# Scores of two 64-dim heads on the two row halves of the matmul array, output products alternating between column halves

## The chip, the cores and the metric

The kernel runs on one core of one Trainium2 chip. The metric is the device time of one execution in microseconds (us). The engines are TensorE (PE: matmuls, with its weight loads listed as PEld), VectorE (DVE), ScalarE (ACT), GpSimd (POOL) and SyncE (SP, which issues most DMAs). TensorE multiplies with an array of 128 rows (the contraction) by 128 columns (the output partitions).

## What is computed

A transformer forward pass on 256 tokens of width 1024: a first block (mixing with attention and long convolutions, then a routed expert layer) and a second one (two layers with two feed-forward parts and one attention each). The change touches the three attentions. All have heads of 64 dimensions, and two heads lie together on 128 partitions. Cut to that:

```python
s = jnp.einsum('bqkgd,btkd->bkgqt', qblk, k) * scale      # mix: 8 query heads, 512 keys
p = softmax(s);  o = jnp.einsum('bkgqt,btkd->bqkgd', p, v)
...
logits = jnp.einsum('bqhmd,bkhmd->bhmqk', qb, k) * scale + bias   # diff: 8 heads, m = 2 maps of 64 dims
w = p[:, :, 0] - lam * p[:, :, 1];  o = jnp.einsum('bhqk,bkhe->bqhe', w, v)
...
logits = jnp.einsum('bqhd,bkhd->bhqk', qb, k) * scale + decay     # forget: 16 heads, causal
p = softmax(logits);  o = jnp.einsum('bhqk,bkhd->bqhd', p, v)
```

## The kernel before, in words

The program runs through nine phases (`PHASES`, line 47): mix, peer, f00, diff, f01, kv, f10, forget, f11. In each the big weights stream in from HBM, are split into a high and a low part (ACT writes `whi`, DVE writes `wlo`), and TensorE multiplies them with the activations, three fp32r products for one exact one (`mm_unit`, line 361). The attention work runs beside this as generators: `spawn` puts one on a list, and `tick`, called twice in each weight unit, takes every generator one step further, to its next `yield`. The framework's scheduler then sets the order of the instructions on each engine, by dependencies and priorities, so neighbours on TensorE need not be neighbours in the code. In the profile and in the orders below, `win`, `qkv`, `bq`, `pacc`, `kvu` and `gu` are such weight products in fp32r; the attention products are fp32. One fp32 product is two TensorE instructions in the trace and one row in the orders.

The attention parts that the change touches:

- `mix` (line 1232), `attn`: four pairs `t` of query heads, two query tiles `qt` of 128. Keys of both heads (256 tokens and 256 context tokens) lie in `kz`, which has one zero-padded copy for each head `m`: rows 0 to 63 hold the keys in copy 0, rows 64 to 127 in copy 1, the rest is zero (memset on POOL, line 1252; filled by `headnorm`, line 1088, in two pieces of 64 partitions). A score `sc` is one product over all 128 rows with 512 output columns. Softmax writes `E`, four transposes write `pt`, ACT copies it to `PT`. The output product `po` takes 64 columns of `V` as weights for each head, so head 0 fills output partitions 0 to 63 and head 1 fills 64 to 127: four products of 256 columns for head 0, then four for head 1.
- `diff` (line 724), `head`: eight heads with two maps `m`. Here the query side is padded: `qz` holds two copies with the other half zero (memsets at line 736, filled by two ACT instructions of 64 partitions for each head). The scores of both maps for one query tile go into one PSUM tile (`ps[:, m]`, from the pool `ps_x`, two buffers); one DVE instruction scales both and adds the bias. Products have 128 (`qt` 0) or 256 (`qt` 1) columns. Its `po` uses the whole array and is not changed.
- `forget` (line 1000), `pair`: eight pairs of heads, padded query copies as in `diff`, one DVE instruction for each head already. `po` has one product of 256 columns and one of 128 for each head, head 0 first.

The two copies with zeros are what lets one head's scores be computed on all 128 rows:

```python
ps = psx.tile([P, 2, nk], F32, tag="s", name="sc")
for m in range(2):
    nc.tensor.matmul(ps[:, m], qz[:, m, qt * P:(qt + 1) * P], k[:, :nk], start=True, stop=True)
```

Of the kernel before, what the change touches and what calls it, by code (L numbers as in the profile page):

```python
# [20 lines left out]
P = 128  # L21
T = 256
# [259 lines left out]
class Kern:  # L282
# [441 lines left out]
    def diff(self):  # L724
# [5 lines left out]
        with ExitStack() as es:  # L730
            pp = es.enter_context(self.tc.tile_pool(name="dfp", bufs=1))
            pw = es.enter_context(self.tc.tile_pool(name="dfw", bufs=2))
            psx = es.enter_context(self.tc.tile_pool(name="ps_x", bufs=2, space=PSUM))
            QZ = [pp.tile([P, 2, T], F32, name=f"qz{j}") for j in range(2)]
            for q in QZ:
                nc.vector.memset(q, 0.0)
            O = pp.tile([P, 2, NH, P], F32, name="O")
            SS = pp.tile([P, 2, NH], F32, name="SS")

            def head(h, qz, k, vf):  # L740
                pv = self.ps_bg.tile([P, 2, P], F32, tag="bg", name="vt")
                for t in range(2):
                    nc.tensor.transpose(pv[:, t], vf[:, t * P:(t + 1) * P], self.ident)
                V = pw.tile([P, 2, P], F32, tag="V", name="V")
                nc.scalar.activation(V, pv, AF.Copy)
                for qt in range(2):
                    nk = (qt + 1) * P
                    ps = psx.tile([P, 2, nk], F32, tag="s", name="sc")
                    for m in range(2):
                        nc.tensor.matmul(ps[:, m], qz[:, m, qt * P:(qt + 1) * P], k[:, :nk], start=True, stop=True)  # L750
                    L = pw.tile([P, 2, nk], F32, tag=f"L{qt}", name="L")
                    bias = self.dbias[:, h, T - nk:]
                    nc.vector.scalar_tensor_tensor(L, ps, 0.125, bias[:, None, :].to_broadcast([P, 2, nk]),
                                                   op0=ALU.mult, op1=ALU.add)
# [24 lines left out]
                    j = pw.tile([P, P], F32, tag="junk", name="junk")  # L779
                    nc.scalar.activation(j, O[:, qt, h], AF.Square, scale=2.0 ** -32, accum_out=SS[:, qt, h:h + 1])  # L780
# [3 lines left out]
            for h in range(NH):  # L784
                t3 = []
                qz = QZ[h % 2]
                for j in range(3):
# [8 lines left out]
                    if j == 0:  # L796
                        if h >= 2:
                            self.drain(*[g for g, n in last if n <= h - 2])
                        for m in range(2):
                            s = slice(m * 64, m * 64 + 64)  # L800
                            nc.scalar.activation(qz[s, m], ps[s], AF.Identity, bias=b[s] if early else 0.0)
                    else:
                        t = pw.tile([P, T], F32, tag=f"kv{j}", name="kvf")
                        if early:
# [195 lines left out]
    def forget(self):  # L1000
# [7 lines left out]
        with ExitStack() as es:  # L1008
            pp = es.enter_context(self.tc.tile_pool(name="fgp", bufs=1))
            pw = es.enter_context(self.tc.tile_pool(name="fgw", bufs=2))  # L1010
            psx = es.enter_context(self.tc.tile_pool(name="ps_x", bufs=2, space=PSUM))
            QZ = [pp.tile([P, 2, T], F32, name=f"qz{j}") for j in range(2)]
            for q in QZ:
                nc.vector.memset(q, 0.0)
            oh, ol = self.hh, self.hl

            def pair(t, qz):
                E2 = [pw.tile([P, 2, (qt + 1) * P], F32, tag=f"E{qt}", name="E") for qt in range(2)]
                for qt in range(2):
                    nk = (qt + 1) * P  # L1020
                    ps = psx.tile([P, 2, nk], F32, tag="s", name="sc")
                    for m in range(2):
                        h = 2 * t + m
                        nc.tensor.matmul(ps[:, m], qz[:, m, qt * P:(qt + 1) * P], self.K[:, t, :nk],
                                         start=True, stop=True)
                    L = pw.tile([P, 2, nk], F32, tag=f"L{qt}", name="L", bufs=1)
                    for m in range(2):
                        h = 2 * t + m
                        nc.vector.scalar_tensor_tensor(L[:, m], ps[:, m], self.F8[:, qt, h:h + 1],
                                                       (self.Fb if qt else self.Fa)[:, h],  # L1030
                                                       op0=ALU.add, op1=ALU.add)
                    sm = pw.tile([P, 8], F32, tag="sm", name="sm", bufs=4)
# [20 lines left out]
                        nc.vector.tensor_copy(WT[:, m], pt)  # L1053
                yield
                po = self.ps_bg.tile([P, T], F32, tag="bg", name="po")
                for m in range(2):
                    h = 2 * t + m
                    s = slice(h * 64, h * 64 + 64)
                    w = WT[:, m].rearrange("p a b -> p (a b)")
                    r = slice(m * 64, m * 64 + 64)  # L1060
                    nc.tensor.matmul(po[r], self.V[:, 0, s], w[:, :T], start=True, stop=False)
                    nc.tensor.matmul(po[r, P:], self.V[:, 1, s], w[:, T:], start=False, stop=True)
                self.split(po, oh[:, t], ol[:, t])
                yield

# [2 lines left out]
            for t in range(8):  # L1068
# [5 lines left out]
                qz = QZ[t % 2]  # L1074
                if t >= 2:
                    self.drain(gens[t - 2])
                for m in range(2):
                    s = slice(m * 64, m * 64 + 64)
                    nc.scalar.activation(qz[s, m], q[s], AF.Identity, bias=b[s])
# [152 lines left out]
    def mix(self):  # L1232
        nc, tc = self.nc, self.tc
        with ExitStack() as es:
# [11 lines left out]
            S = self.S = Stream(self, make_plan(self.phases),  # L1246
                                [k.rearrange("p a b c -> p (a b c)") for k in (self.KR, self.KS)])
            nc.sync.dma_start(self.X, self.ins["xT"])
            kz = pm.tile([P, 2, 2 * T], F32, name="kz")
            V = pm.tile([P, 4, P], F32, name="Vt")  # L1250
            Q = pm.tile([P, 4, T], F32, name="Q")
            nc.gpsimd.memset(kz, 0.0)
            zs = pm.tile([P, 12, T], F32, name="zs")
            with ExitStack() as e2:
                pc = e2.enter_context(tc.tile_pool(name="mixctx", bufs=1))
# [50 lines left out]
                for n, j in enumerate(WORD):  # L1306
                    w = S.take("win", n)
                    for i, x in enumerate((H, HC)):
# [4 lines left out]
                        ps = self.ps_mm.tile([P, T], F32, tag="mm", name="win")  # L1313
                        self.mm_unit(ps, w, x)
                        if j == 4:
                            first(self.headnorm(pw, ps, self.col("kg"), i == 0, [(slice(m * 64, m * 64 + 64),
                                                  kz[m * 64:m * 64 + 64, m, i * T:(i + 1) * T]) for m in range(2)]))
# [28 lines left out]
            def attn():  # L1346
                for t in range(4):
                    PT = [pa.tile([P, 4, 2, P], F32, tag=f"PT{m}", name="PT", bufs=1) for m in range(2)]
                    for m in range(2):
                        for qt in range(2):  # L1350
                            ps = psx.tile([P, 2 * T], F32, tag="s", name="sc")
                            nc.tensor.matmul(ps, Q[:, t, qt * P:(qt + 1) * P], kz[:, m], start=True, stop=True)
                            sm = pa.tile([P, 4], F32, tag="sm", name="sm", bufs=4)
                            nc.vector.tensor_reduce(sm[:, 0:1], ps, axis=AX.X, op=ALU.max)
                            nc.vector.tensor_scalar(sm[:, 1:2], sm[:, 0:1], -0.125, None, op0=ALU.mult)
# [2 lines left out]
                            nc.scalar.activation(E, ps, AF.Exp, scale=0.125, bias=sm[:, 1:2], accum_out=sm[:, 2:3])  # L1358
                            nc.vector.reciprocal(sm[:, 3:4], sm[:, 2:3])
                            nc.vector.tensor_scalar(E, E, sm[:, 3:4], None, op0=ALU.mult)  # L1360
                            yield
                            pt = self.ps_bg.tile([P, 4, P], F32, tag="bg", name="pt")
                            for k in range(4):
                                nc.tensor.transpose(pt[:, k], E[:, k * P:(k + 1) * P], self.ident)
                            nc.scalar.activation(PT[m][:, :, qt], pt, AF.Copy)
                    yield
                    po = self.ps_bg.tile([P, T], F32, tag="bg", name="po")
                    for m in range(2):
                        r = slice(m * 64, m * 64 + 64)
                        for k in range(4):  # L1370
                            nc.tensor.matmul(po[r], V[:, k, r], PT[m][:, k].rearrange("p a b -> p (a b)"),
                                             start=k == 0, stop=k == 3)
                    self.split(po, xh[:, t], xl[:, t])
                    yield

# [655 lines left out]
```

## Time and profile before

| what | value |
|---|---|
| median of 3 runs | 2221.97 us (2220.69 to 2222.41) |
| the profiled execution's own time | 2221.92 us |
| its span, first to last instruction | 2220.1 us |
| TensorE busy | 2176.8 us, 98% |
| DVE busy | 1706.2 us, 77% |
| ACT busy | 1150.0 us, 52% |
| chain that ended last | PE 86%, DVE 8%, ACT 3%, DMA 3% |

The page's busy share of TensorE counts modelled ends, and matmuls overlap in it; so a distance between two recorded starts tells more of a matmul's price than its listed duration. The three touched stretches lie at about 105 to 250 us (mix), 1385 to 1492 us (diff) and 1950 to 2011 us (forget).

### The profile page before, as it was taken

Reading aid. Unit: us, or ns where it says so; the run is one execution under the profiler, and the core shown is the slowest. Engines: PE = TensorE matmul, PEld = TensorE weight load, DVE = VectorE, ACT = ScalarE, POOL = GpSimd, SP = SyncE. Lnnn points to the kernel's source line nnn. Section 1 sums busy time; section 2 is a strip of 40 time slices with the busy share of each in tenths; the row PEclk is TensorE's granted clock in tenths of the full one; section 3 lists DMA queues with packets and bytes.
Section 4 is the critical chain, followed back from the end, with each engine's and each line's share of the span. In section 5 each row is a group of like instructions: output and inputs, shape, how many; then the busy total and the mean of one; then the engine's idle time right before and its main releaser. Section 6 shows DMA issues by size and latency. Waiting matters only on the chain.

```text
span 2220.1 us, 41653 instructions
## 1 busy us (share of the span) xinstructions
PE 2176.8 (98%) x17298; PEld 2091.2 (94%) x17298; DVE 1706.2 (77%) x3056; ACT 1150.0 (52%) x1788; POOL 10.9 (0%) x25
## 2 busy tenths in 40 slices
PE   7999999999999999999999899999999999999998
PEld 4887999999889999999999899999999999999998
DVE  7789689887996777567777687878776887798554
ACT  5677565454334444444455345766445544476443
POOL 0000000000000000000000000000000000000000
PEclk9999999999999999999999999999999999999999
DMA  8256344544349888557776875436784688724551
GB/s 317 77 188 221 126 180 152 190 176 185 124 152 274 303 304 297 198 204 271 291 286 193 323 307 225 146 141 225 299 305 165 228 323 313 273 96 171 190 180 49
DMA packets 100605, 481.20 MB, mean 217 GB/s; under 512 B 40808, under 2 KB 41336, under 8 KB 44928
## 3 DMA queue, kind: packets, MB, share of 16 engines
q1 hardware_dynamic: 95744, 462.70, 57.4%
q10 hardware_dynamic: 3456, 10.90, 1.3%
q0 software_dynamic: 1216, 4.94, 1.0%
q8 instruction: 136, 2.23, 0.4%
q14 instruction: 53, 0.43, 0.1%
HBM read 467.48 MB, written 11.03 MB: 216 GB/s over the span
## 4 chain that ended last, share of the span: by engine, by line
PE 86%; DVE 8%; ACT 3%; DMA 3%; issue 1%; SPq 0%; DVEq 0%; ACTq 0%
PE acc L263 27%; PE gu L263 19%; PE u L263 15%; PE win L263 4%; DMA raw<-wts 3%; PE qkv L263 2%; PE gux L263 2%; DVE wlo L263 2%; PE pacc L263 2%; PE kvu L263 2%; PE gps L263 2%; PE ss L263 2%; PE sc L263 1%; DVE A L263 1%; PE po L263 1%; ACT whi L263 1%
## 5 line engine op out<-in xcount | busy, mean ns | idle before, releaser
L263 DVE TENSOR_TENSOR wlo<-raw,whi 128x1024 fp32r<-128x1024 f32 x650 | 792.6, 1222 | 302.8 <-ACT whi L263 301.0
L263 ACT ACTIVATE whi<-raw 128x1024 fp32r<-128x1024 f32 x650 | 684.3, 1055 | 498.2 <-PE acc L263 128.1
L263 PE MATMUL gu<-hh,wlo 128*128 128x256 f32 x1264 | 309.9, 283 | 0.0
L263 PE MATMUL gu<-hh,whi 128*128 128x256 f32 x1264 | 309.8, 283 | 0.0
L263 PE MATMUL acc<-wh,whi 128*128 128x256 f32 x1024 | 289.8, 283 | 0.0
L263 PE MATMUL acc<-wh,wlo 128*128 128x256 f32 x1024 | 289.8, 283 | 0.0
L263 PE MATMUL acc<-wl,whi 128*128 128x256 f32 x1024 | 289.8, 283 | 0.0
L263 DVE SCALAR_TENSOR_TENSOR junk<-raw,crow 128x1024 f32<-128x1024 f32 x198 | 241.7, 1220 | 47.4 <-DMA raw<-wts 38.6
L263 PE MATMUL u<-hh,whi 128*128 128x256 f32 x1024 | 253.7, 284 | 3.4 <-ACT whi L263 3.4
L263 PE MATMUL u<-hh,wlo 128*128 128x256 f32 x1024 | 253.1, 285 | 2.1 <-DVE wlo L263 2.1
L263 PEld LDWEIGHTS gu<-hh,whi 128*128 128x128 f32 x1264 | 241.5, 191 | 0.0
L263 PEld LDWEIGHTS gu<-hh,wlo 128*128 128x128 f32 x1264 | 241.5, 191 | 0.0
L263 PE MATMUL acc<-ah,whi 128*128 128x256 f32 x704 | 198.5, 282 | 6.7 <-ACT ah L263 6.7
L263 PEld LDWEIGHTS u<-hh,whi 128*128 128x128 f32 x1024 | 196.4, 192 | 5.1 <-ACT whi L263 5.1
L263 PEld LDWEIGHTS u<-hh,wlo 128*128 128x128 f32 x1024 | 196.2, 192 | 5.2 <-DVE wlo L263 4.0
L263 PE MATMUL acc<-al,whi 128*128 128x256 f32 x704 | 198.7, 283 | 0.8 <-DVE al L263 0.8
L263 PE MATMUL acc<-ah,wlo 128*128 128x256 f32 x704 | 197.0, 280 | 0.0
L263 PEld LDWEIGHTS acc<-wh,whi 128*128 128x128 f32 x1024 | 196.6, 192 | 0.0
L263 PEld LDWEIGHTS acc<-wh,wlo 128*128 128x128 f32 x1024 | 196.6, 192 | 0.0
L263 PEld LDWEIGHTS acc<-wl,whi 128*128 128x128 f32 x1024 | 196.6, 192 | 0.0
L263 PE MATMUL gu<-hl,whi 128*128 128x256 f32 x1264 | 177.4, 283 | 0.0
L263 PEld LDWEIGHTS gu<-hl,whi 128*128 128x128 f32 x1264 | 163.0, 191 | 0.0
(393 smaller groups left out, 4034.2 us busy)
## 6 DMA issues: line engine op xcount, KB each, us to landing
raw<-wts SPq DMA_DIRECT2D x427, 1024.0 KB, 4.9
G<-sp ACTq DMA_DIRECT2D x16, 512.0 KB, 2.6
gl<-G SPq DMA_DIRECT2D x16, 512.0 KB, 7.0
Fb<-fscr POOLq DMA_DIRECT2D x1, 2048.0 KB, 9.5
scr<-vec POOLq DMA_DIRECT2D x1, 1536.0 KB, 36.9
KR<-wts SPq DMA_DIRECT2D x1, 1024.0 KB, 11.1
KS<-wts SPq DMA_DIRECT2D x1, 1024.0 KB, 12.8
X<-xT SPq DMA_DIRECT2D x1, 1024.0 KB, 14.8
```

Source lines behind the costliest of these rows:

```text
L263: i = f(*a, **kw)
```

## The change

The zero padding goes. `kz` and `qz` become one copy with both heads, head 0 on rows 0 to 63 and head 1 on rows 64 to 127; the memsets go; ACT fills `qz` in one instruction instead of two, `headnorm` writes `kz` in one piece instead of two. A score now takes only the 64 rows of its head, and the scores of the two heads go to two PSUM tiles (`pss`), both buffers of the tag `s`. In `diff` the one DVE instruction on both maps becomes two. In `mix` the loop over heads moves inside the loop over query tiles, and both heads' scores are issued before the first softmax. The output products of `mix` and `forget` alternate between head 0 and head 1 (column halves), key block by key block.

```diff
@@ diff
-            QZ = [pp.tile([P, 2, T], F32, name=f"qz{j}") for j in range(2)]
-            for q in QZ:
-                nc.vector.memset(q, 0.0)
+            QZ = [pp.tile([P, T], F32, name=f"qz{j}") for j in range(2)]
...
-                    ps = psx.tile([P, 2, nk], F32, tag="s", name="sc")
-                    for m in range(2):
-                        nc.tensor.matmul(ps[:, m], qz[:, m, qt * P:(qt + 1) * P], k[:, :nk], start=True, stop=True)
+                    pss = [psx.tile([P, nk], F32, tag="s", name="sc") for _ in range(2)]
+                    for m, ps in enumerate(pss):
+                        s = slice(m * 64, m * 64 + 64)
+                        nc.tensor.matmul(ps, qz[s, qt * P:(qt + 1) * P], k[s, :nk], start=True, stop=True)
...
-                    nc.vector.scalar_tensor_tensor(L, ps, 0.125, bias[:, None, :].to_broadcast([P, 2, nk]),
-                                                   op0=ALU.mult, op1=ALU.add)
+                    for m, ps in enumerate(pss):
+                        nc.vector.scalar_tensor_tensor(L[:, m], ps, 0.125, bias, op0=ALU.mult, op1=ALU.add)
...
-                        for m in range(2):
-                            s = slice(m * 64, m * 64 + 64)
-                            nc.scalar.activation(qz[s, m], ps[s], AF.Identity, bias=b[s] if early else 0.0)
+                        nc.scalar.activation(qz, ps, AF.Identity, bias=b if early else 0.0)
@@ forget (its qz, its scores and its ACT instruction change as in diff)
...
-                for m in range(2):
-                    h = 2 * t + m
-                    s = slice(h * 64, h * 64 + 64)
-                    w = WT[:, m].rearrange("p a b -> p (a b)")
-                    r = slice(m * 64, m * 64 + 64)
-                    nc.tensor.matmul(po[r], self.V[:, 0, s], w[:, :T], start=True, stop=False)
-                    nc.tensor.matmul(po[r, P:], self.V[:, 1, s], w[:, T:], start=False, stop=True)
+                for k in range(2):
+                    for m in range(2):
+                        h = 2 * t + m
+                        s = slice(h * 64, h * 64 + 64)
+                        w = WT[:, m].rearrange("p a b -> p (a b)")
+                        r = slice(m * 64, m * 64 + 64)
+                        nc.tensor.matmul(po[r, k * P:], self.V[:, k, s], w[:, k * T:T + k * P], start=k == 0,
+                                         stop=k == 1, skip_group_check=True)
@@ mix
-            kz = pm.tile([P, 2, 2 * T], F32, name="kz")
+            kz = pm.tile([P, 2 * T], F32, name="kz")
...
-            nc.gpsimd.memset(kz, 0.0)
...
-                    for m in range(2):
-                        for qt in range(2):
-                            ps = psx.tile([P, 2 * T], F32, tag="s", name="sc")
-                            nc.tensor.matmul(ps, Q[:, t, qt * P:(qt + 1) * P], kz[:, m], start=True, stop=True)
+                    for qt in range(2):
+                        pss = [psx.tile([P, 2 * T], F32, tag="s", name="sc") for _ in range(2)]
+                        for m, ps in enumerate(pss):
+                            r = slice(m * 64, m * 64 + 64)
+                            nc.tensor.matmul(ps, Q[r, t, qt * P:(qt + 1) * P], kz[r], start=True, stop=True)
+                        Es = []
+                        for m, ps in enumerate(pss):
...
+                            Es.append(E)
                             yield
+                        for m, E in enumerate(Es):
...
-                    for m in range(2):
-                        r = slice(m * 64, m * 64 + 64)
-                        for k in range(4):
+                    for k in range(4):
+                        for m in range(2):
+                            r = slice(m * 64, m * 64 + 64)
                             nc.tensor.matmul(po[r], V[:, k, r], PT[m][:, k].rearrange("p a b -> p (a b)"),
-                                             start=k == 0, stop=k == 3)
+                                             start=k == 0, stop=k == 3, skip_group_check=True)
```

The scheduler also sets a new order. Three places of TensorE's order matter below. In the rows, the name before the arrow is what is written, the names behind it are the operands, then come the output's partitions and columns; `xN` stands for N equal rows. A score row (`sc`) of the change takes 64 rows of the array, a `po` row 64 columns, all other rows the whole array.

First place: TensorE in `diff`, scores of the first head for the second query tile, of the kernel before.

```order
L263 MATMUL qkv<-xg_13152,whi 128x258
L263 MATMUL qkv<-xg_13152,wlo 128x258
L263 MATMUL qkv<-xg_13152,whi 128x258
L263 MATMUL sc<-kvf,qz_15625 128x256
L263 MATMUL qkv<-xg_13152,wlo 128x258
L263 MATMUL sc<-kvf,qz_15625 128x256
L263 MATMUL qkv<-xg_13152,whi 128x258
```

The same place in the change:

```order
L263 MATMUL qkv<-xg_13149,whi 128x258
L263 MATMUL qkv<-xg_13149,wlo 128x258
L263 MATMUL qkv<-xg_13149,whi 128x258
L263 MATMUL sc<-kvf,qz_15622 128x256
L263 MATMUL qkv<-xg_13149,wlo 128x258
L263 MATMUL sc<-kvf,qz_15622 128x256
L263 MATMUL qkv<-xg_13149,whi 128x258
```

The order did not move here: a weight product still stands between the two scores, which now belong to different row halves.

Second place: TensorE in `forget`, the output products `po` of the first pair of heads, with the scores (`sc`) and transposes (`wt`) about them, of the kernel before.

```order
L263 MATMUL sc<-K,qz_22696 128x256 x2
L263 MATMUL bq<-xg_13153,whi 128x258 x3
L263 MATMUL po<-WT,V 64x256
L263 MATMUL po<-WT,V 64x128
L263 MATMUL po<-WT,V 64x256
L263 MATMUL po<-WT,V 64x128
L263 MATMUL wt<-cols,E 128x128
```

The same products in the change:

```order
L263 MATMUL sc<-K,qz_22715 128x128
L263 MATMUL bq<-xg_13149,wlo 128x258
L263 MATMUL po<-WT,V 64x256
L263 MATMUL bq<-xg_13149,whi 128x258
L263 MATMUL bq<-xg_13149,wlo 128x258
L263 MATMUL bq<-xg_13149,whi 128x258
L263 MATMUL bq<-xg_13149,wlo 128x258
L263 MATMUL bq<-xg_13150,whi 128x258 x4
L263 MATMUL po<-WT,V 64x256
L263 MATMUL po<-WT,V 64x128 x2
```

Before, the four products stand together. Now head 0's first one stands alone, and eight weight products come before the other three.

Third place: TensorE in `mix`, the output products of the first pair of heads, with convolution products (`U`) and transposes (`pt`), of the kernel before.

```order
L263 MATMUL U<-uT,mixc 128x512 x2
L263 MATMUL pt<-cols,E 128x128 x4
L263 MATMUL po<-PT,Vt 64x256 x8
L263 MATMUL U<-uT,mixc 128x512 x2
L263 MATMUL win<-hh,whi 128x256
```

The same in the change:

```order
L263 MATMUL win<-hl,whi 128x256 x8
L263 MATMUL po<-PT,Vt 64x256 x3
L263 MATMUL U<-uT,mixc 128x512 x2
L263 MATMUL po<-PT,Vt 64x256 x5
L263 MATMUL sc<-kz,Q 128x512 x2
L263 MATMUL U<-uT,mixc 128x512 x2
```

The eight products are now cut in two by `U`, and the next two scores follow them directly, side by side.

## Rows read from the trace of the kernel before

**Rows 1.** The page: span, and part 1, busy time, share and instructions of each engine.

```profile
span 2220.1 us, 41653 instructions
...
PE 2176.8 (98%) x17298; PEld 2091.2 (94%) x17298; DVE 1706.2 (77%) x3056; ACT 1150.0 (52%) x1788; POOL 10.9 (0%) x25
```

**Rows 2.** Busy time in stretches: start:end, length, engines, PEclk, DMA share, GB/s.

```profile
105.00:250.00 145.00, 144.28 (x886) 114.70 (x885) 117.73 (x229) 102.96 (x154) 0.10 (x1) 1.00 0.49 178
1385.00:1415.00 30.00, 29.92 (x239) 29.07 (x238) 29.05 (x80) 23.20 (x58) 0.00 (x0) 1.00 0.44 162
...
1950.00:1985.00 35.00, 34.85 (x269) 31.55 (x268) 31.56 (x100) 27.99 (x72) 0.00 (x0) 1.00 0.26 93
```

**Rows 3.** Timeline of TensorE, mix: start us, length us, engine, line, instruction, xcount.

```profile
105.49 1.02 PE L263 MATMUL sc<-kz,Q 128*128 128x512 f32 x2
106.35 0.59 PE L263 MATMUL hn_ps<-hn_sq,mixc 128*128 128x256 f32 x2
106.78 0.59 PE L263 MATMUL hn_ps<-hn_g,mixc 128*128 128x256 f32 x2
```

**Rows 4.** Timeline of TensorE in mix, output products: both halves, then one alone.

```profile
167.45 2.86 PE L263 MATMUL po<-PT,Vt 128*64 128x256 f32 x16
170.24 1.98 PE L263 MATMUL U<-uT,mixc 128*128 128x512 f32 x4
...
219.07 1.94 PE L263 MATMUL po<-PT,Vt 128*64 128x256 f32 x8
220.94 0.38 PE L263 MATMUL win<-hh,whi 128*128 128x256 f32 x1
```

**Rows 5.** Timeline of TensorE in forget, output products among whole-array products.

```profile
1993.94 0.28 PE L263 MATMUL pacc<-hh,whi 128*128 128x256 f32 x1
1994.16 0.88 PE L263 MATMUL po<-WT,V 128*64 128x256 f32 x8
...
1995.18 0.28 PE L263 MATMUL pacc<-hl,whi 128*128 128x256 f32 x1
1995.30 0.28 PE L263 MATMUL pacc<-hh,whi 128*128 128x256 f32 x1
```

**Rows 6.** Timeline of TensorE: one-column products `kn` in mix among whole-array products.

```profile
129.20 0.28 PE L263 MATMUL win<-hh,wlo 128*128 128x256 f32 x1
129.41 1.88 PE L263 MATMUL kn<-fkt,mixc 128*1 128x512 f32 x4
...
131.44 0.28 PE L263 MATMUL win<-hh,wlo 128*128 128x256 f32 x1
```

**Rows 7.** Timeline of TensorE in kv: a product on 16 rows (`lft`).

```profile
1715.34 0.29 PE L263 MATMUL lft<-cols,lf 16*128 16x16 f32 x2 [0.49 <-DVE lf L263]
1715.56 0.39 PE L263 MATMUL kvu<-xg,whi 128*128 128x258 f32 x1
1715.78 0.28 PE L263 MATMUL kvu<-xg,wlo 128*128 128x258 f32 x1
```

**Rows 8.** Timeline of TensorE in kv: 16-column products (`fgp`), their end.

```profile
1708.81 0.28 PE L263 MATMUL fgp<-xg,fl 128*16 128x258 f32 x1
1708.93 0.28 PE L263 MATMUL kvu<-xg,whi 128*128 128x258 f32 x1
```

**Rows 9.** Tiles `sc` and `qz`: instructions, min/median/max ns, first and last start.

```profile
L263 DVE SCALAR_TENSOR_TENSOR L<-sc,dbias x16: 418/549/692, 1390.3 to 1474.6; 128x256 f32<-128x256 f32 x8, 128x512 f32<-128x512 f32 x8
L263 DVE SCALAR_TENSOR_TENSOR L<-sc,F,Fa x16: 330/342/351, 1952.9 to 1995.9; 128x128 f32<-128x128 f32 x16
L263 DVE SCALAR_TENSOR_TENSOR L<-sc,F,Fb x16: 461/476/480, 1953.4 to 1999.8; 128x256 f32<-128x256 f32 x16
...
L263 ACT ACTIVATE qz<-fix,fixb x22: 492/503/511, 1387.3 to 1985.1; 64x256 f32<-64x256 f32 x22
L263 ACT ACTIVATE qz<-qkv x10: 364/379/381, 1417.0 to 1466.1; 64x256 f32<-64x256 f32 x10
L263 DVE MEMSET qz<- x4: 485/485/485, 1159.0 to 1754.5; 128x512 f32 x4
```

More of the change, by code (lines that the diff above doesn't have):

```diff
@@ L1011, in forget @@
             psx = es.enter_context(self.tc.tile_pool(name="ps_x", bufs=2, space=PSUM))
-            QZ = [pp.tile([P, 2, T], F32, name=f"qz{j}") for j in range(2)]
-            for q in QZ:
-                nc.vector.memset(q, 0.0)
+            QZ = [pp.tile([P, T], F32, name=f"qz{j}") for j in range(2)]
             oh, ol = self.hh, self.hl
@@ L1020, in pair @@
                     nk = (qt + 1) * P
-                    ps = psx.tile([P, 2, nk], F32, tag="s", name="sc")
-                    for m in range(2):
-                        h = 2 * t + m
-                        nc.tensor.matmul(ps[:, m], qz[:, m, qt * P:(qt + 1) * P], self.K[:, t, :nk],
-                                         start=True, stop=True)
+                    pss = [psx.tile([P, nk], F32, tag="s", name="sc") for _ in range(2)]
+                    for m, ps in enumerate(pss):
+                        s = slice(m * 64, m * 64 + 64)
+                        nc.tensor.matmul(ps, qz[s, qt * P:(qt + 1) * P], self.K[s, t, :nk], start=True, stop=True)
                     L = pw.tile([P, 2, nk], F32, tag=f"L{qt}", name="L", bufs=1)
@@ L1028, in pair @@
                         h = 2 * t + m
-                        nc.vector.scalar_tensor_tensor(L[:, m], ps[:, m], self.F8[:, qt, h:h + 1],
+                        nc.vector.scalar_tensor_tensor(L[:, m], pss[m], self.F8[:, qt, h:h + 1],
                                                        (self.Fb if qt else self.Fa)[:, h],
@@ L1055, in pair @@
                 po = self.ps_bg.tile([P, T], F32, tag="bg", name="po")
-                for m in range(2):
-                    h = 2 * t + m
-                    s = slice(h * 64, h * 64 + 64)
-                    w = WT[:, m].rearrange("p a b -> p (a b)")
-                    r = slice(m * 64, m * 64 + 64)
-                    nc.tensor.matmul(po[r], self.V[:, 0, s], w[:, :T], start=True, stop=False)
-                    nc.tensor.matmul(po[r, P:], self.V[:, 1, s], w[:, T:], start=False, stop=True)
+                for k in range(2):
[6 more added lines that the diff above has]
+                                         stop=k == 1, skip_group_check=True)
                 self.split(po, oh[:, t], ol[:, t])
@@ L1076, in forget @@
                     self.drain(gens[t - 2])
-                for m in range(2):
-                    s = slice(m * 64, m * 64 + 64)
-                    nc.scalar.activation(qz[s, m], q[s], AF.Identity, bias=b[s])
+                nc.scalar.activation(qz, q, AF.Identity, bias=b)
                 self.tick()
@@ L1315, in mix @@
                         if j == 4:
-                            first(self.headnorm(pw, ps, self.col("kg"), i == 0, [(slice(m * 64, m * 64 + 64),
-                                                  kz[m * 64:m * 64 + 64, m, i * T:(i + 1) * T]) for m in range(2)]))
+                            first(self.headnorm(pw, ps, self.col("kg"), i == 0, [(allr, kz[:, i * T:(i + 1) * T])]))
                         elif j == 5:
@@ L1348, in attn @@
                     PT = [pa.tile([P, 4, 2, P], F32, tag=f"PT{m}", name="PT", bufs=1) for m in range(2)]
-                    for m in range(2):
-                        for qt in range(2):
-                            ps = psx.tile([P, 2 * T], F32, tag="s", name="sc")
-                            nc.tensor.matmul(ps, Q[:, t, qt * P:(qt + 1) * P], kz[:, m], start=True, stop=True)
+                    for qt in range(2):
[4 more added lines that the diff above has]
+                        Es = []
+                        for m, ps in enumerate(pss):
                             sm = pa.tile([P, 4], F32, tag="sm", name="sm", bufs=4)
@@ L1367, in attn @@
                     po = self.ps_bg.tile([P, T], F32, tag="bg", name="po")
-                    for m in range(2):
-                        r = slice(m * 64, m * 64 + 64)
-                        for k in range(4):
+                    for k in range(4):
+                        for m in range(2):
+                            r = slice(m * 64, m * 64 + 64)
                             nc.tensor.matmul(po[r], V[:, k, r], PT[m][:, k].rearrange("p a b -> p (a b)"),
-                                             start=k == 0, stop=k == 3)
+                                             start=k == 0, stop=k == 3, skip_group_check=True)
                     self.split(po, xh[:, t], xl[:, t])
```

## The prediction

> **What bounds the kernel now.** I read the page's first parts, then the busy time of the three touched stretches, then TensorE's timeline inside them, then the instructions on the tiles `sc` and `qz`. TensorE is the bound: 98% of a span of 2220.1 us [rows 1]. In the touched stretches it is denser still, 144.28 of 145 us in mix, 29.92 of 30 early in diff, 34.85 of 35 early in forget, at a granted clock of 1.00, which is the 2.4 GHz level [rows 2]. So what TensorE gains or loses there the span gains or loses. DVE comes next, 29.05 of 30 us early in diff and 31.56 of 35 early in forget; ACT has 23.20 and 27.99 there.
>
> Prices on TensorE are distances between starts. An fp32 product of 256 columns takes 0.43 us (106.35 to 106.78), one of 512 columns 0.86 (105.49 to 106.35) [rows 3]; by columns, 0.215 for 128 is my estimate. A whole-array weight product takes 0.12 (1995.18 to 1995.30) [rows 5].
>
> Do two halves of the array work beside one another? Column halves do. Four products on one half alone, 4 x 0.43 = 1.72 of work, last 1.87 us until the next product (219.07 to 220.94), but both halves together, eight products, only 2.79 (167.45 to 170.24) [rows 4], though head 0's four come first in the order. In forget the four products of a pair hold 2 x 0.43 + 2 x 0.215 = 1.29 of work and are over in less [rows 5], so there the halves already overlap fully, 0.645 for both.
>
> **A visit to a smaller tile has a price.** Take the weight product before such a visit and the second one behind it: between their starts lie the visit's work, two ordinary steps of 0.12, and the price. In forget that is 1995.18 - 1993.94 = 1.24; less 0.645 and 0.24 this leaves 0.35 us [rows 5]. For `kn`, one column wide, 131.44 - 129.20 = 2.24, less 4 instructions of 0.43 and 0.24, leaves 0.28 [rows 6]. One half alone shows 1.87 - 1.72 = 0.15 behind its first start [rows 4]. No row of this trace uses 64 rows with 128 columns. The nearest by shape is `lft` on 16 rows: 0.44 from its first start to the second weight product behind it, of which 0.03 is work (16 columns twice) and 0.12 a step, so 0.29, and its entry is hidden in a wait [rows 7]. But `fgp`, 16 columns wide, pays nothing: 0.12 from its last start to the next weight product [rows 8]. So the ends for a visit to a row half are 0 (`fgp`) and 0.40 (`lft`'s 0.29 and the part of 0.35 that lies before and at the entry, about 0.1). I take 0.35: `po` and `lft` agree with it, and both cut the array at 64 columns or along the rows, as the change does.
>
> The Trainium skill, "TensorEngine Tiling (Array Packing)", section "Key Properties", speaks against the change here: a change of the tiling mode, not just of the tile, drains TensorE. By that rule every visit to a row half pays; by `fgp`'s row none would, and the sum below would be -5.5 us instead of +14.8. The trace agrees with the rule in `po` and `kn` (0.35 and 0.28) and not in `fgp`.
>
> **The change, part by part.**
>
> *Overlap of scores.* Two scores can overlap only if nothing that uses the whole array stands between them. That is read off TensorE's order for all 40 pairs: 8 in mix, 16 in diff, 16 in forget. Neighbours are 4 in mix (512 columns), 8 in diff (seven of 128, one of 256) and 6 in forget (one of 128, five of 256). The other 22 have weight products, transposes or `po` between the two heads, as in the first place shown. A neighbouring pair saves one of its two products: 4 x 0.86 + 6 x 0.43 + 8 x 0.215 = 7.7 us. That takes row halves to overlap like column halves; the other end is 0.
>
> *Output products.* In mix a block of eight takes 2.79 - 0.15 = 2.64 three times, and once its halves stand apart, 3.44: 11.4. In the change the eight are cut 3 + 5, 1 + 7, 1 + 7 and 8; a piece lasts as long as its fuller half: (0.86 + 1.29) + 2 x (0.43 + 1.72) + 1.72 = 8.2. That saves 3.2 us. In forget nothing was left to gain, and in six of eight pairs the first product now stands alone (second place shown), 0.43 more each: it costs 2.6 us.
>
> *Visits.* In the order before, 13 stretches of `po` leave the whole array (5 in mix, 8 in forget); the scores leave it never. In the change scores do so in 62 stretches (18 pairs and 44 single ones) and `po` in 21 (7 in mix, 14 in forget). Eight times one follows the other directly, which joins two visits. So there are 75 visits, 62 more: 62 x 0.35 = 21.7 us. The eight changes inside a visit I put at half a visit, 0.17: 1.4 us (ends 0 and 0.35 each).
>
> *Other engines.* DVE: 16 instructions of 0.42 or 0.68 us on both maps become 16 of 0.34 and 16 of 0.48, by forget's rows of the same shapes [rows 9]: 16 x 0.34 + 16 x 0.48 - 8 x 0.42 - 8 x 0.68 = +4.3 us in diff. Early in diff, where DVE has 0.95 of 30 us free, three heads add 1.6, but TensorE grows there by three neighbouring pairs (0.35 - 0.215 each) and six single visits (0.35), 2.5 in all, which covers it; uncovered, it would cost up to 1.6. ACT loses 16 of 32 instructions of 0.38 to 0.50 [rows 9], some 7.4 us; DVE loses four memsets of 0.485 and two pieces of `kz`, POOL one memset. I put these at nothing, for TensorE's own work runs over them; were any on the path, the change would gain by it, at most those 7.4 and 4 x 0.485 = 1.9.
>
> *Waits.* Both PSUM tiles of the tag `s` now belong to one pair, so the next pair waits until DVE has read both. Behind it on TensorE stand all weight products. Each such wait is between 0 and one DVE instruction of 0.34 longer than before, on 16 places in diff and forget: 0 to 5.4 us. I take 0: several weight products stand between most pairs.
>
> Sum: -7.7 - 3.2 + 2.6 + 21.7 + 1.4 = **+14.8 us**, made against the profiled execution's own 2221.92 us (span 2220.1 and 1.8 around it), within 0.1 us of the median of 2221.97. That gives **2236.7 us**, 0.7% slower. By stage: mix 18 visits instead of 5, -3.4 - 3.2 + 4.6 + 0.2 = about -2; diff 24 instead of none, -2.0 + 8.4 = +6; forget 33 instead of 8, -2.4 + 2.6 + 8.8 + 1.2 = +10.
>
> **The rivals.**
>
> *Row halves cost no visit.* If a row half costs nothing, as `fgp`, what is left is -7.7 - 3.2 + 2.6 and eight more `po` visits, 2.8: -5.5 us, **2216.4**, faster. It decides below about 0.10 us for a visit: the 54 visits that scores add meet the -5.5 there. For it speaks `fgp` alone, against it `lft`, which also cuts the rows. Chance 0.08. A half price, 0.17, gives -5.5 + 54 x 0.17 = +3.7, 2225.6, inside 0.2%: chance 0.07.
>
> *Row halves do not overlap.* Then 7.7 us more: **2244.4**. For it: no row shows two row halves at work. Against it: column halves overlap down to 0.645 of 1.29. Chance 0.13.
>
> *A wait takes the place of the work removed.* The two PSUM tiles are freed late, because DVE is at 31.56 of 35 us in forget: up to 5.4 more, **2242**. Against it: the order puts weight products between. Chance 0.12.
>
> *The change doesn't do what it says.* In 22 of 40 pairs it does not, since the two halves never meet on TensorE; this is in the sum already.
>
> **How the numbers follow.** The forecast (a visit at 0.30 to 0.40) has 0.60. A measurement here can tell about 0.2%, 4.4 us: faster means below 2217.5, slower above 2226.4. Slower: 0.60 + 0.13 + 0.12 = 0.85; same: 0.07; faster: 0.08. For the range I leave out the free visit and the far end of "no overlap" with waits on top, and keep the half price's upper part: 2226 to 2247.
>
> **What would show it right or wrong.** In TensorE's timeline of the changed kernel a score alone between weight products should take, from the product before it to the second behind it, 0.35 more than its work and two steps; a neighbouring pair of 512 columns should take about 0.86 instead of 1.72 in all. `po` in mix should be over in about 1.9 us where all eight stand together. The stretches should differ by about -2 (mix), +6 (diff) and +10 (forget) us. A score between weight products without extra distance would make the prediction wrong, as would DVE as the named releaser of idle TensorE time in forget.

## The result, and the profile after

The changed kernel took **2236.88 us** (median of 6 runs, 2236.21 to 2240.68) against 2221.14 us for the kernel before, timed beside it (6 runs, 2220.69 to 2222.41). The ratio is 1.0073 (95% interval 1.006 to 1.0085): slower, at the predicted size.

The page of the changed kernel, its span and the first line of part 1, answers to [rows 1]:

```profile
span 2234.4 us, 41647 instructions
...
PE 2190.9 (98%) x17298; PEld 2086.3 (93%) x17298; DVE 1705.0 (76%) x3066; ACT 1137.8 (51%) x1768; POOL 9.9 (0%) x24
```

TensorE issues the same 17298 matmuls and is busy 14.1 us longer; the span is 14.3 us longer. The other engines have a little less to do. The busy time of the stretches of [rows 2] (start:end, length, then PE, PEld, DVE, ACT and POOL, granted clock, DMA share, GB/s):

```profile
105.00:250.00 145.00, 144.24 (x899) 111.91 (x898) 119.10 (x230) 98.50 (x153) 0.17 (x2) 1.00 0.49 178
1385.00:1415.00 30.00, 30.00 (x223) 26.65 (x222) 27.49 (x75) 20.55 (x52) 0.00 (x0) 1.00 0.46 169
1950.00:1985.00 35.00, 35.00 (x228) 27.55 (x228) 29.02 (x78) 20.99 (x49) 0.00 (x0) 1.00 0.34 121
```

TensorE is just as full at the same clock of 1.00, but fewer matmuls fit in: 223 instead of 239 in 30 us of diff, 228 instead of 269 in 35 us of forget (227 in a window moved by the 5 us that forget starts later). DVE and ACT are less busy there than before, so neither became the bound. TensorE's timeline of the changed kernel shows where the time goes (start us, length us, engine, line, instruction, xcount; a group's instructions start 0.12 apart where they are weight products):

```profile
219.28 0.88 PE L263 MATMUL win<-hl,whi 128*128 128x256 f32 x6
220.09 1.13 PE L263 MATMUL sc<-kz,Q 64*128 64x512 f32 x4
221.15 0.39 PE L263 MATMUL win<-hh,whi 128*128 128x256 f32 x1
221.38 0.28 PE L263 MATMUL win<-hh,wlo 128*128 128x256 f32 x1
...
243.95 1.95 PE L263 MATMUL po<-PT,Vt 128*64 128x256 f32 x16
245.83 0.39 PE L263 MATMUL win<-hh,whi 128*128 128x256 f32 x1
...
1436.92 0.28 PE L263 MATMUL qkv<-hh,whi 128*128 128x256 f32 x1
1437.13 0.49 PE L263 MATMUL sc<-kvf,qz 64*128 64x128 f32 x4
1437.56 0.38 PE L263 MATMUL qkv<-hh,wlo 128*128 128x256 f32 x1
1437.78 0.28 PE L263 MATMUL qkv<-hh,whi 128*128 128x256 f32 x1
...
1959.44 0.28 PE L263 MATMUL bq<-xg,wlo 128*128 128x258 f32 x1
1959.65 0.49 PE L263 MATMUL sc<-K,qz 64*128 64x128 f32 x2
1960.07 0.40 PE L263 MATMUL bq<-xg,whi 128*128 128x258 f32 x1
1960.30 0.28 PE L263 MATMUL bq<-xg,wlo 128*128 128x258 f32 x1
```

Read it as the prediction did, from the weight product ahead to the second one behind. A lone score of 128 columns (two instructions, last four rows) takes 1960.30 - 1959.44 = 0.86 us. Less 0.215 of work and two steps of 0.12, the **visit costs 0.40**. A neighbouring pair of them (four instructions, 1436.92 to 1437.78) takes 0.86 as well: the second head's score is free, so row halves overlap fully. The pair of 512 columns says the same: the last of six `win` products starts at 219.28 + 5 x 0.12 = 219.88, the second behind the scores at 221.38, and 1.50 - 0.86 - 0.24 leaves 0.40, where two scores on the whole array would hold 1.72 of work. A whole block of eight `po` is over in 1.88 us (243.95 to 245.83), against 2.79 in [rows 4].

The table cuts each profiled execution into stages, at the first starts of the products `fkp` (66.3 us in the kernel before), `outs` (251.7), `qkv` (1377.0), `kvu` (1694.0), `bq` (1940.7) and the last start of `pacc` (2014.8), and gives by how much a stage is longer than before (us). In the changed kernel they add up to the span's +14.3.

| kernel | to fkp (start) | to outs (mix) | to qkv | to kvu (diff) | to bq | to pacc (forget) |
|---|---|---|---|---|---|---|
| changed kernel | +1.48 | -1.47 | +0.46 | +4.16 | -0.03 | +9.77 |
| scores alone | +2.56 | -0.64 | +0.49 | +4.16 | -0.04 | +9.32 |
| output products alone | +0.11 | -2.07 | +0.11 | +0.05 | +0.01 | -0.03 |
| pairs kept together | +0.66 | -4.70 | +0.30 | -0.17 | -0.01 | -0.49 |
| one visit for a head pair | +2.93 | -4.90 | +0.33 | -2.20 | +1.18 | -2.51 |
| mix alone, pairs kept | +2.58 | -4.59 | +0.43 | +0.06 | -0.01 | +0.04 |
| changed, fill kept | -1.20 | -1.50 | +0.37 | +4.13 | -0.01 | +9.76 |
| one visit, fill kept | -0.42 | -5.12 | +0.23 | -2.19 | -0.03 | -2.56 |
| mix alone, fill kept | -0.98 | -5.03 | +0.20 | +0.07 | -0.02 | 0.00 |

### The profile page after: what moved, and what is told of

It reads as the page before. It is cut to its first block, busy times and chain, and to the rows that moved or that the text cites. A ratio compares the mean times of both kernels' runs of the same rounds, so it can differ in the third digit from the quotient of the medians.

```text
span 2234.4 us, 41647 instructions
## 1 busy us (share of the span) xinstructions
PE 2190.9 (98%) x17298; PEld 2086.3 (93%) x17298; DVE 1705.0 (76%) x3066; ACT 1137.8 (51%) x1768; POOL 9.9 (0%) x24
## 4 chain that ended last, share of the span: by engine, by line
PE 90%; DVE 6%; DMA 2%; ACT 2%; issue 1%; DVEq 0%; ACTq 0%
PE acc L263 27%; PE gu L263 19%; PE u L263 16%; PE win L263 4%; PE qkv L263 3%; PE gux L263 2%; PE pacc L263 2%; DMA raw<-wts 2%; PE kvu L263 2%; PE sc L263 2%; PE gps L263 2%; PE ss L263 2%; DVE wlo L263 1%; PE po L263 1%; PE bq L263 1%; PE outs L263 1%
```

## Experiments

**1. Scores alone.** The output products go back to head 0 first.

```diff
-                    for k in range(4):
-                        for m in range(2):
-                            r = slice(m * 64, m * 64 + 64)
+                    for m in range(2):
+                        r = slice(m * 64, m * 64 + 64)
+                        for k in range(4):
...
```

> The change with the output products of mix and forget put back to head 0 first, then head 1. Theory (each stretch of TensorE's order that leaves the whole array has a price, about 0.39 us for a row half by the changed kernel's timeline, and only neighbouring scores overlap): the scores still make 62 such stretches, 18 of them pairs, and the output products 17; streams fall by 6.0 us and visits cost some 24 more: +15 to +18 us against the kernel before. Rival A (the new order of the output products makes the loss): within 4 us of the kernel before. Rival B (waits on the two PSUM tiles and the split DVE instruction make the loss): about +15 as well, with DVE named behind TensorE's idle time.

Measured: 2237.60 us, ratio 1.007 (1.0054 to 1.0085). The loss is all there without the alternating order; diff (+4.16) and forget (+9.32) are as in the changed kernel.

**2. Output products alone.** Padded copies and scores as before, `po` alternating.

> The kernel before with only the output products of mix and forget alternating between the heads. Theory: three more stretches that leave the whole array (16 instead of 13), streams 2.6 us shorter, so -1.5 us (-3 to +0.5). Rival A (this order makes the loss): +8 us or more. Rival B says nothing of it: 0.

Measured: 2220.28 us, ratio 0.9992 (0.9983 to 1.0001). Mix gains 2.07 us in the profile, forget nothing: there all eight `po` blocks stay whole, as before. The time alone can't tell this from no change.

**3. Pairs kept together.** Both heads' scores write one PSUM tile of two banks and get a priority that keeps them neighbours (`po` also starts with head 1).

```diff
-                    pss = [psx.tile([P, nk], F32, tag="s", name="sc") for _ in range(2)]
+                    p2 = psx.tile([P, 2, 512], F32, tag="s", name="sc", bufs=1)
+                    pss = [p2[:, m, :nk] for m in range(2)]
+                    with self.tc.high_priority(offset=400):
...
```

> The change with the scores of two heads kept next to each other on TensorE: one PSUM tile of two banks instead of two tiles, a high scheduling priority for the scores, and head 1 ahead of head 0 in the output products so that these don't start before both heads are ready. Theory: 40 score stretches, all of them pairs, and 13 of output products; streams 21.5 us shorter, visits 14.4 dearer: -7 us against the kernel before (-10 to -3). Rival B (PSUM waits): the two banks are now freed only together, after both DVE instructions, so it stays at +12 us or more.

Measured: 2217.97 us, ratio 0.9982 (0.9973 to 0.9991). All 40 pairs are neighbours, so there are 40 stretches of scores instead of 62, and the loss of diff and forget is gone (-0.17, -0.49). With one PSUM tile between a pair and the next, waits for DVE would be longer than in the changed kernel; the kernel is faster all the same, so waits are not what the change lost by. A wait of another kind shows behind the scores in mix (TensorE's timeline of this run):

```profile
153.29 1.13 PE L263 MATMUL sc<-kz,Q 64*128 64x512 f32 x4
156.30 0.63 PE L263 MATMUL pt<-cols,E 128*128 128x128 f32 x4 [1.89 <-DVE E L263]
```

The transposes wait 1.89 us for the softmax of a pair that now comes at once.

**4. The price by itself.** Scores, `po` and padding as before; 72 products of 128 columns on constants are added between feed-forward weight products, 18 for each of four shapes. Their results are not used.

```diff
+                        if j == 0 and f >= 4:
+                            r, c = {"f00": (P, 16), "f01": (64, P), "f10": (P, 64), "f11": (P, P)}[ph]
+                            nc.tensor.matmul(self.ps_bg.tile([P, T], F32, tag="bg", name="try")[:c, :P],
+                                             self.ident[:r, :c], self.ident[:r], start=True, stop=True)
```

> The kernel before with 72 extra small products of 128 fp32 columns, 18 in each feed-forward part, each alone between two weight products, with its result unused: 128 rows by 16 columns in the first, 64 by 128 in the second, 128 by 64 in the third, 128 by 128 in the fourth. From the weight product before to the second behind it there lie two steps of 0.12 us and 0.215 of work. Theory: the rest is 0.39 for 64 rows, 0.35 for 64 columns, 0 for the whole array, and 0 for 16 columns as in the kernel before; so 18 x 4 x 0.215 = 15.5 us of work and 13.3 of visits, +29 us in all. Rival (a visit is free, the loss in the attentions has another cause): 0 for all four, +15.5 us in all. If 16 columns pay as well, +34.

Measured: one run, span 2250.9 us, +30.8. TensorE's timeline of this run: 64 rows, then the whole array.

```profile
1600.23 0.76 PE L263 MATMUL gu<-hl,whi 128*128 128x256 f32 x5
1600.92 0.48 PE L263 MATMUL try<-cols 64*128 64x128 f32 x2
1601.34 0.39 PE L263 MATMUL gu<-hh,whi 128*128 128x256 f32 x1
1601.56 0.28 PE L263 MATMUL gu<-hh,wlo 128*128 128x256 f32 x1
...
2132.26 0.88 PE L263 MATMUL gu<-hl,whi 128*128 128x256 f32 x6
2132.98 0.38 PE L263 MATMUL try<-cols 128*128 128x128 f32 x2
2133.11 0.36 PE L263 MATMUL gu<-hh,whi 128*128 128x256 f32 x1
2133.32 0.28 PE L263 MATMUL gu<-hh,wlo 128*128 128x256 f32 x1
```

For 64 rows the last `gu` starts at 1600.23 + 4 x 0.12 = 1600.71, the second behind at 1601.56: 0.85, less 0.215 and 0.24, is **0.39**, the scores' price. The whole array pays nothing (2133.32 - 2132.86 = 0.46, all work and steps). In the same way 64 columns pay 0.34 and 16 columns 0.30, for which 0 was expected; all 18 products of a shape agree within 0.01. So the price comes with the tile's size and not with a stray fp32 product.

**5. One visit for a head pair.** In diff and forget both query tiles' scores of a pair stand together (four products, one visit), and diff's two DVE instructions are one again; mix as in 3.

```diff
+                    for qt in range(2):
+                        for m in range(2):
+                            s = slice(m * 64, m * 64 + 64)
+                            nc.tensor.matmul(p2[:, m, qt * P:qt * P + (qt + 1) * P], qz[s, qt * P:(qt + 1) * P],
...
```

> As the kernel with the pairs kept together, but in diff and forget all four scores of a head pair (both query tiles) are issued next to each other into one two-bank PSUM tile, so that one stay on the row halves serves 0.645 us of work for each half: 24 score stretches instead of 40. Theory: 16 stays fewer at 0.39 us, 6.2 us less than with the pairs kept, of which some will vanish in waits: -7 to -12 us against the kernel before, about -9. Rival (the attentions' chain of softmax steps, not the price of stays, sets what is left): no better than with the pairs kept, -4 us.

Measured: 2215.88 us, ratio 0.9973 (0.9962 to 0.9983). Diff and forget now gain 2.20 and 2.51 us, as fewer visits should; less is gained in all than expected, with +2.93 at the start and +1.18 in kv, where TensorE waits 1.2 us once for ACT (`vf`).

**6. Mix alone, pairs kept.** Diff and forget as before; the `po` of mix gets the priority too.

> diff and forget as in the kernel before; only mix takes row halves, pairs kept together, and alternating output products. Theory: eight pairs of 512 columns save 0.86 - 0.39 us each, 3.8 in all, and four blocks of output products 3.2: -7 us at most, of which 4.7 were measured in this stage with the pairs kept: -5 us (-8 to -3). Rival (only long runs inside one stay pay, pairs don't): 0.

Measured: 2221.13 us, ratio 0.9997 (0.9988 to 1.0006). Mix gains 4.59 us as expected, and the start loses 2.58. Here the start became a question: every kernel without the zero fill of `kz` loses there.

**7 to 9. The fill put back.** A tile of the old size is zeroed on POOL again and one half of it used; in the changed kernel, in 5 and in 6.

```diff
-            kz = pm.tile([P, 2 * T], F32, name="kz")
+            kz2 = pm.tile([P, 2, 2 * T], F32, name="kz")
+            kz = kz2[:, 0]
...
+            nc.gpsimd.memset(kz2, 0.0)
```

> The changed kernel with the one zero fill of the keys' tile on POOL put back (tile of the old size, only one half used); nothing else differs. In the runs so far every kernel without this fill reached its first product `win` 0.4 to 2.9 us later than before (changed kernel +1.5), and every kernel with it within 0.3. Theory: without the fill the scheduler orders DVE's instructions at the start another way, and that is the +1.5. With it back, DVE's first 33 instructions stand in the old order, `win` starts within 0.3 us of before, and the span is about 1.5 us shorter than the changed kernel's 2234.4, 2233. Rival: the start is late because of the different tiles or of chance in the DMAs; then `win` stays 1 us or more late, and the time stays at 2234.4 in the span.

> The version in which both heads' scores stay neighbours in all three attentions and forget's output products keep one visit, with the zero fill put back. Without the fill it took 0.9973 of before, of which its start took +2.9 us. Theory: the start comes back to within 0.3 us of before, so 2.5 us less than without the fill: span about 2212.3, ratio about 0.996. Rival (the start does not hang on the fill): 0.9973 again.

> Paired scores and alternating output products in mix alone, zero fill put back. Without the fill mix gained 4.6 us and the start lost 2.6, and the time was unchanged within its interval. Theory: the start is back, and the gain of mix is seen in the time: -4.6 us, ratio 0.998. Rival: the time stays at 0.9997.

Measured: the changed kernel with the fill 2235.38 us, ratio 1.0062 (1.0048 to 1.0076); one visit with the fill **2211.96 us, ratio 0.9955 (0.9942 to 0.9969)**, the fastest of all and faster than both kernels; mix alone with the fill 2219.19 us, 0.9986 (0.9977 to 0.9995). DVE's first 33 instructions stand in the old order in all three, as the theory had it, but that order is not what costs the time. ACT makes two copies (`zs`) of a TensorE result early in the program, and a reduction (`junk`) on DVE reads the second one. The timelines of ACT, DVE and TensorE show them, first of the kernel before, then of the changed one, then of the changed one with the fill:

```profile
9.25 0.60 ACT L263 ACTIVATE zs<-crow_ps 128x512 f32<-128x512 f32 x1 [0.77 <-PE crow_ps L263]
10.14 0.60 ACT L263 ACTIVATE zs<-crow_ps 128x512 f32<-128x512 f32 x1 [0.30 <-PE crow_ps L263]
...
10.77 1.23 DVE L263 SCALAR_TENSOR_TENSOR junk<-raw,zs 128x1024 f32<-128x1024 f32 x1 [1.02 <-ACT zs L263]
...
39.70 0.38 PE L263 MATMUL win<-hh,whi 128*128 128x256 f32 x1 [0.42 <-ACT hh L263]
```

```profile
9.58 0.60 ACT L263 ACTIVATE zs<-crow_ps 128x512 f32<-128x512 f32 x1 [1.11 <-PE crow_ps L263]
10.20 1.28 ACT L263 ACT_TABLE_LOAD   x1
11.49 0.51 ACT L263 ACTIVATE decay<-tau,cols 128x256 f32<-128x256 f32 x1
11.91 0.58 ACT L263 ACTIVATE zs<-crow_ps 128x512 f32<-128x512 f32 x1
...
12.52 1.23 DVE L263 SCALAR_TENSOR_TENSOR junk<-raw,zs 128x1024 f32<-128x1024 f32 x1 [2.78 <-ACT zs L263]
...
41.29 0.58 PE L263 MATMUL win<-hh,whi 128*128 128x256 f32 x1
```

```profile
8.43 0.60 ACT L263 ACTIVATE zs<-crow_ps 128x512 f32<-128x512 f32 x1 [0.30 <-PE crow_ps L263]
9.38 0.60 ACT L263 ACTIVATE zs<-crow_ps 128x512 f32<-128x512 f32 x1 [0.35 <-PE crow_ps L263]
...
10.01 1.23 DVE L263 SCALAR_TENSOR_TENSOR junk<-raw,zs 128x1024 f32<-128x1024 f32 x1 [0.61 <-ACT zs L263]
...
38.62 0.58 PE L263 MATMUL win<-hh,whi 128*128 128x256 f32 x1
```

Without the fill, ACT loads a table and does a first `decay` between the two copies, so they start 2.33 us apart instead of 0.89. DVE waits 2.78 instead of 1.02 us for the second one, and its reduction starts 1.75 us later. DVE's own order differs only from its 31st instruction on (the reciprocal `rstd` stands ahead of the last two reductions instead of the last one). There, at about 30 us, the last reduction starts 1.83 us later (32.25 instead of 30.42): nearly all of this delay was 20 us old. The first `win` comes 1.59 us later. With the fill all are back, even 0.8 to 1.1 us earlier than before, where the theory said within 0.3.

The two copies start 2.32 to 2.33 us apart in all five kernels without the fill, and 0.89 to 0.99 in all six with it (with the kernel before and the price run). So ACT's order goes with the fill, and without it the second copy is held up by about 1.4 us. Why the scheduler changes that order is not shown; POOL's `tau`, which `decay` reads, starts 1.0 us earlier without the fill.

In all ten other profiles the stage to `fkp` is longer without the fill (+0.66 to +2.93, five kernels) than with it (-1.20 to +0.28, five with the price run). In the three that lose most, experiments 1, 5 and 6, TensorE also waits 4.6 to 5.6 us for the DMA of `hf`, in all others 1.1 to 2.4; whether that belongs to the fill is not settled. The medians fall by 1.50, 3.92 and 1.94 us with it; since the intervals of each two versions overlap, the size is uncertain (of the 3.92, up to 1.2 can be the wait in kv of experiment 5); the direction is the same three times.

## Why the prediction was right, and where it was not

The time was met (2236.7 forecast, 2236.88 measured), and for the reason given, but terms that it had wrong cancel: the three touched stages give +12.5 together, and +1.9 comes from stages that the forecast left alone.

- **The visit.** Taken at 0.35, with ends 0 and 0.40; it costs 0.39 to 0.40, in scores and alone (experiment 4). `lft` and `po` were the right neighbours, `fgp` the wrong one. So the rivals of a free and of a half-price visit fall. A change between scores and `po` inside a visit, taken at 0.17, measures 0.16: in experiment 8 2.09 us lie between the product ahead and the second one behind such a visit, and 2 x 0.645 of work, two steps and one visit of 0.40 are 1.93. The Trainium skill, "TensorEngine Tiling (Array Packing)", section "Key Properties", says that a change of tiling mode drains TensorE; for 64 rows the trace agrees, at those 0.39 us a visit.
- **Overlap.** Taken as full for 18 pairs; it is full (0.86 with one score or with two). The rival without overlap falls. Experiment 3 turns the argument round: with all 40 pairs neighbours the loss of diff and forget is gone.
- **Output products.** In mix the alternation alone gains 2.07. In experiment 2 all four blocks are cut 1 + 7. By the prediction's prices that saves 11.4 - 4 x 2.15 = 2.8 us of work, and three more visits leave 1.75 of it; the method holds. In forget the forecast's +2.6 belongs to cuts inside the blocks of four products, and I put these down to the alternating order. That was half right: with the old order and the new scores the blocks are cut too (12 stretches in experiment 1, 14 in the changed kernel, 8 before), and the alternation without the new scores cuts none.
- **Stages.** Mix -1.47 (about -2 forecast), forget +9.77 (+10). Diff, +4.16 instead of +6, is the first mis-sized term. With 0.40 for a visit it should even have been 24 x 0.40 - 2.0 = +7.6. What was left out is time that TensorE already lost beside the scores before. The kernel before, TensorE's timeline at the place that answers to 1436.92 above:

```profile
1433.22 0.39 PE L263 MATMUL po<-V,WT 128*128 128x128 f32 x2
1433.71 0.71 PE L263 MATMUL sc<-kvf,qz 128*128 128x128 f32 x4
1434.18 0.36 PE L263 MATMUL qkv<-hh,wlo 128*128 128x256 f32 x1
1434.38 0.28 PE L263 MATMUL qkv<-hh,whi 128*128 128x256 f32 x1
```

The second `po` instruction starts 0.11 behind the first, at 1433.33, and the scores 0.38 later, though it holds 0.11 of work. From there to the second `qkv` it is 1.05 us, in the changed kernel 0.86: the visit is paid, and the place is still shorter. Three heads show this, with 0.38 to 0.45 ahead of the scores. That is some 1.2 us (3 x about 0.4) of the 3.4 by which +7.6 was missed. Read like this at all scores of diff, TensorE loses 1.7 us beside them in the kernel before and 9.7 in the changed one, so the 24 visits did cost their 24 x 0.40. The other 1.9 of the 3.4 were saved away from the scores, by a cause that is not settled.
- **The start.** For POOL's memset among others the prediction said "I put these at nothing" and "were any on the path, the change would gain by it"; that is the step that failed: the change lost 1.5 us there in the profile. What mattered was not the fill's own time (0.95 us on POOL) but that without it the scheduler put ACT's instructions at the start in another order, which makes DVE wait 1.8 us longer for `zs`. The order is set before a run; the prediction looked only at the three attentions. So +1.5 not foreseen and 2 too much in diff make the sum good, and that is luck.
- **Other engines and waits.** No wait on DVE took the place of the work removed: TensorE is busy 30.00 of 30 and 35.00 of 35 us, TensorE's trace shows no wait in forget and 0.8 us of waits in all of diff (1.0 before), and DVE is less busy than before. The tile rows of the changed kernel (min/median/max ns) answer to [rows 9]:

```profile
L263 DVE SCALAR_TENSOR_TENSOR L<-sc,dbias x32: 269/348/426, 1390.5 to 1480.0; 128x128 f32<-128x128 f32 x16, 128x256 f32<-128x256 f32 x16
...
L263 ACT ACTIVATE qz<-fix,fixb x11: 491/510/513, 1387.8 to 1997.0; 128x256 f32<-128x256 f32 x11
L263 ACT ACTIVATE qz<-qkv x5: 378/385/392, 1421.0 to 1470.0; 128x256 f32<-128x256 f32 x5
```

The split DVE instruction costs 0.27 to 0.43 each, less than the 0.34 and 0.48 that I took, and ACT fills both heads in the time that one half took.

What the version with one visit does differently is seen in forget (TensorE's timeline of experiment 8):

```profile
1959.19 0.72 PE L263 MATMUL bq<-xg,whi 128*128 128x258 f32 x4
1959.85 0.93 PE L263 MATMUL sc<-K,qz 64*128 64x128 f32 x8
1960.70 0.87 PE L263 MATMUL po<-WT,V 128*64 128x256 f32 x8
1961.50 0.39 PE L263 MATMUL bq<-xg,wlo 128*128 128x258 f32 x1
```

Four scores (eight instructions, 2 x 0.215 + 2 x 0.43 = 1.29 us of work on the whole array) and four output products stand in one stretch and are over in 1.65 us, 1959.85 to 1961.50. Forget has 16 score stretches in experiment 3, 8 here, and 26 in the changed kernel.

## What to carry to other kernels

Cutting the array pays by the stretch, not by the product: each stay on 64 rows among whole-array products cost 0.39 us here, and a pair saves one of its two products only if the two are neighbours on TensorE, so a lone score always loses and a pair of 128 columns (0.215 saved) too; a pair of 256 (0.43) about breaks even. Check in the scheduled order that the halves meet, and if they don't, tie them together (one PSUM tile for both, a priority, several pairs in one stay) before the padding goes. And read the order of the whole program, not of the touched stage alone: taking away a fill at the start moved ACT's work there, some 95 us ahead of the first score.

## What the runs showed of the hardware that was not expected

- A small tile's price depends on its shape: 0.39 us for 64 rows, 0.34 for 64 columns, 0.30 for 16 columns, 0.005 for the whole array (experiment 4). Yet `fgp`, 16 columns too, pays nothing [rows 8].
- The weight loads (PEld) tell the two kinds apart. First two loads of experiment 4, for the 64-row product and for the `gu` behind it; then the load for the whole-array product of that run; then, in the kernel before, the load for the `kvu` behind `fgp`:

```profile
1600.92 0.29 PEld L263 LDWEIGHTS try<-cols 64*128 64x128 f32 x2
1601.33 0.19 PEld L263 LDWEIGHTS gu<-hh,whi 128*128 128x128 f32 x1
...
2132.86 0.31 PEld L263 LDWEIGHTS try<-cols 128*128 128x128 f32 x2
...
1708.81 0.19 PEld L263 LDWEIGHTS kvu<-xg,whi 128*128 128x128 f32 x1
```

Among whole-array products a load starts with the product ahead of its own (2132.86, its product at 2132.98), and beside `fgp` as well (1708.81, its product at 1708.93). At a visit it does not: the load of 1600.92 starts 0.21 us behind the start of the product ahead (1600.71) and at once with its own product, and so does the `gu` load of 1601.33. All 54 visits to a smaller tile in experiment 4 show this, on the way in and on the way out. `fgp` is fp32r and the products of experiment 4 are fp32; why its loads can run ahead no run shows.
- The 18 visits on 16 columns lengthened their stage by 7.3 us, less than 18 x (0.215 + 0.30) = 9.3. TensorE was idle 17.4 us of that stage in the kernel before and 15.2 in this run, so the other 2 us fell into waits that were there already.
- The Trainium skill, "TensorEngine Tiling (Array Packing)", section "Theoretical Speedup", gives up to 2 times for a dimension of 64 or less. Two neighbouring scores reach that in their work (0.215 for both instead of 0.43), but with the visit the pair takes 0.86 - 0.24 = 0.62 us, longer than the 0.43 on the whole array.
